# Attention probabilities of one head in four transposed by TensorE in float32, instead of by DMA in float16

## Chip, core and metric

One core of a Trainium2 chip runs the whole kernel. The metric is the device time of one execution in microseconds (us), the median over several runs. "TensorE" is the matmul engine (PE in the profile, PEld its weight loads), VectorE is DVE, ScalarE is ACT, GpSimd is POOL; SP is the engine whose queue issues most DMAs (SPq).

## What is computed

One layer of a hybrid encoder block in float32: 1024 tokens and 16 meta tokens of width 1024. Two groups of heads run beside each other, a gated delta-net (a chain over chunks of tokens, forward and backward) and attention with 8 query heads of width 64 on 2 key/value heads. Their outputs go through one output projection, a norm and an MLP of width 4096. Of the attention, which the change touches, the reference says:

```python
def attend(qb):
    s = jnp.einsum('bqhgd,bkhd->bhgqk', qb, k, preferred_element_type=jnp.float32)
    p = jax.nn.softmax(s, axis=-1).astype(v.dtype)
    return jnp.einsum('bhgqk,bkhd->bqhgd', p, v)

u = rms_norm(h, norm_mix_pre[l])
proj = u @ w_in[l]
o_dn = gated_deltanet_group(dq, dk, dv, dz, db, da, ...)
o_at = axial_gqa_group(aq, ak, av, q_norm[l], k_norm[l])
mix = jnp.concatenate([o_dn, o_at], axis=-1) @ w_out[l]
h = h + rms_norm(mix, norm_mix_post[l])
```

The chip computes float32 products from pairs of a high and a low part, so that most operands exist twice.

## The kernel before

The attention works through 64 heads: 8 tiles of 128 queries, 8 heads in each; `j` is a head's place in its group of four (`g, j = divmod(h, 4)`).

- **Scores** (`qk_head`): four matmuls of 512 columns (two halves of the keys, each with KH and KL) into one of two score buffers `S` of two PSUM banks. VectorE takes the extreme of each row (L1254) and forms the bias `nb` (L1255). The score buffer is free once ScalarE has taken the exponentials out of it.
- **Softmax** (`softmax`): ScalarE writes the exponentials of a head as float32 into `p32`, a tile `t` of a ring of four (L1262), and those of the meta keys into `pm` (L1265). It casts them to float16 into `P16` (L1268); GpSimd subtracts for the first 640 columns (L1270) and VectorE for the rest (L1271) to get the low part. Then SP issues one DMA transpose of both parts into `pT` (L1274): 8 blocks of 128x128 for the high part, 8 for the low. There are four `P16` and three `pT`.
- **Weighted sum** (`pv_head`): 24 matmuls with blocks of `pT` as weights into the accumulator `o`. For the last head of each group, the meta keys' part and the division follow, and `AQ` takes the result.

Beside this stand, one after the other, the delta-net chain (`chain`: matmuls on `st`, `rr`, `tt`, `at`, `kd`), the load and split of the output projection's weights (`wout_stream`), and the projection itself (`proj_stream`: `mix` transposes a tile of both groups' outputs, then 48 matmuls of 512 columns on `wob*` and `woa*`). All these take PSUM banks from one pool `a` of three (`psr`); the scores and `o` have their own five.

The order of all this isn't written out by hand. Each stage is a generator; `progress` runs them against a clock `T.t` that counts planned TensorE time (a transpose adds 0.1 us, a matmul its columns). `yield 2.0` means "not before 2 us of planned time later", and of those due the one first in `URGENCY` goes. So a matmul or transpose that is added anywhere moves what comes behind it on all engines. Each engine then runs its own instructions strictly in that order. In planned time, the weighted sum of a head is due `TP_` = 13.8 after its scores, and the steps of `softmax` are `SM` = 1.46, 1.4, 0.7 and 2.0 apart.

Of the kernel before, what the change touches and what calls it, by code (L numbers as in the profile page):

```python
# [8 lines left out]
F16 = mybir.dt.float16  # L9
# [4 lines left out]
ALU = mybir.AluOpType  # L14
AX = mybir.AxisListType
P = 128
# [8 lines left out]
NQ = 8  # L25
# [45 lines left out]
INF, P16N = 6, 4  # L71
# [4 lines left out]
AB, GB, SB, PTB = 3, 5, 2, 3  # L76
# [5 lines left out]
def body(tc, I, out, dbg=None):  # L82
    nc = tc.nc
    V, A, G, S = nc.vector, nc.scalar, nc.gpsimd, nc.sync
# [3 lines left out]
    class Clock:  # L88

        t = 0.0  # L90
# [10 lines left out]
    T = Clock()  # L101
# [10 lines left out]
    def tmp(dt=F32):  # L112
        return tp.tile([P, LT + 4], dt, name="t4", tag="t4")

    def psr():
        return psa.tile([P, 512], F32, name="a", tag="a")

    def ps1():
        return (R["g"] or psa).tile([P, 512], F32, name="a", tag="a")
# [13 lines left out]
    def v3(ap, m=P):  # L133
        return ap.rearrange("p (h c) -> p h c", c=m)

    def cload(name, pool=cp):
        at, n = WHERE[name]
        t = pool.tile([P, n], F32, name="c_" + name, tag="c_" + name, bufs=1)
        S.dma_start(t, cst[:, at:at + n])
        return t  # L140
# [32 lines left out]
    R = dict(g=psg)  # L173
# [472 lines left out]
    idf = cload("id")  # L646
# [16 lines left out]
    ps = ps1()  # L663
# [579 lines left out]
    def qk_head(t, h, qs, sm, mm, box):  # L1243
        kv = h // 4
        ap_, KH, KL = R["at"], R["KH"], R["KL"]
        s = R["ps"].tile([P, L], F32, name="S", tag="S", bufs=SB)
        for half in range(2):
            sl = slice(half * 512, (half + 1) * 512)
            for i, K_ in enumerate((KH, KL)):
                T.matmul(s[:, sl], lhsT=qs[:, h], rhs=K_[:, kv, sl], start=i == 0, stop=i == 1)  # L1250
            if half == 0:
                yield
        mx, nb = small(1, "mx"), small(1, "nb")
        V.tensor_reduce(mx, s, AX.X, ALU.min)  # L1254
        V.tensor_scalar(nb, mx, mm[:, h:h + 1], UP15, ALU.min, ALU.add)  # L1255
        spawn("post", softmax(t, h, s, sm, nb, box))
        yield

    def softmax(t, h, s, sm, nb, box):
        yield SM[0]  # L1260
        p32 = tmp()
        A.activation(p32[:, :L], s, AF.Exp, bias=nb, scale=-1.0)  # L1262
        g, j = divmod(h, 4)
        pm = R["PM"][(2 * t + g) % 3]
        A.activation(pm[:, j * NM:(j + 1) * NM], sm[:, h * NM:(h + 1) * NM], AF.Exp, bias=nb, scale=-1.0)  # L1265
        yield SM[1]
        p16 = R["P16"][(t * NQ + h) % P16N]
        A.copy(p16[:, 0], p32[:, :L])  # L1268
        yield SM[2]
        G.tensor_tensor(p16[:, 1, :LH], p32[:, :LH], p16[:, 0, :LH], ALU.subtract)  # L1270
        V.tensor_tensor(p16[:, 1, LH:], p32[:, LH:L], p16[:, 0, LH:], ALU.subtract)  # L1271
        yield SM[3]
        pT = R["at"].tile([P, 16, P], F16, name="pT", bufs=PTB)
        S.dma_start_transpose(pT, p16.rearrange("p a b -> p (a b)"))  # L1274
        box[h] = pT
        if j == 3:
            ps = psr()[:, :P]
            T.transpose(ps, pm, idf)
            mh, ml = (R["at"].tile([P, P], F16, name=n, bufs=2) for n in ("pmh", "pml"))
            A.copy(mh, ps)  # L1280
            V.tensor_tensor(ml, ps, mh, ALU.subtract)
            box["m", g] = mh, ml
# [608 lines left out]
```

## Time and profile before

| | before |
|---|---|
| median of 3 runs | 1414.7 us (1414.13 to 1419.95) |
| the profiled execution | 1416.07 us, its span 1414.2 us |
| TensorE busy | 1342.7 us, 95% of the span |
| VectorE, ScalarE, GpSimd busy | 1029.3, 835.5, 295.4 us |
| attention in the trace | scores from 435.8 us on, last weighted sum until 745.5 us |
| end of the delta-net chain, start of the projection's matmuls | 582.7 us, 623.7 us |

Busy time of an engine is the time in which it executes; TensorE's matmuls overlap, and their ends are modelled, so that the distance from one start to the next says more than a duration. The time from one engine's wait to another's end is read from rows of the timeline, and "idle <- X" in such a row means that the engine stood until X was done. A DMA share over 1 means that packets of several transfers overlapped on the 16 rings.

### The profile page before, as it was taken

The page shows a single profiled execution, that of the slowest core. Times are in us where ns is not written, and L with a number is a line of the kernel's source. Part 1 is how long each engine was busy: PE and PEld are TensorE (multiplying, and loading weights), DVE is VectorE, ACT ScalarE, POOL GpSimd, SP SyncE. Part 2 cuts the span into 40 slices and gives each one's busy share as a digit, 9 for nine tenths or more (in the row PEclk, how much of TensorE's full clock was granted, in tenths as well). Part 3 has the DMA queues.
Part 4 walks back from the last instruction along what each step waited for, and adds up shares of the span by engine and source line. Part 5 has one row for each costly group of instructions (what it writes and reads, how often), then busy time and mean ns, then how long its engine had stood idle before and what let it go on. Part 6 is the DMA issues. An engine that isn't in the chain of part 4 may idle for free. (4 is left out here: it accounts for less than half of the span.)

```text
span 1414.2 us, 26476 instructions
## 1 busy us (share of the span) xinstructions
PE 1342.7 (95%) x9627; PEld 1027.1 (73%) x9627; DVE 1029.3 (73%) x1962; ACT 835.5 (59%) x1747; POOL 295.4 (21%) x386
## 2 busy tenths in 40 slices
PE   6999999999998998899998799999999999999996
PEld 6999888777998877677777444444444888888875
DVE  5636779788768979877765987777775588675675
ACT  6556565756546777866644676666665455445552
POOL 1210234343534456533321200000000000000000
PEclk9999999999998999889999799999999999999998
DMA  6312234344379999997994354444443984466341
GB/s 209 87 57 62 83 98 158 112 149 153 121 253 282 245 264 239 221 242 186 224 225 135 102 175 158 153 155 150 158 155 114 331 271 127 142 193 194 98 150 66
DMA packets 273355, 236.86 MB, mean 167 GB/s; under 512 B 147484, under 2 KB 201656, under 8 KB 273224
## 3 DMA queue, kind: packets, MB, share of 16 engines
q1 hardware_dynamic: 270056, 225.73, 55.3%
q10 hardware_dynamic: 3168, 9.44, 1.8%
q8 instruction: 76, 1.25, 0.4%
q14 instruction: 55, 0.45, 0.1%
HBM read 132.27 MB, written 69.28 MB: 143 GB/s over the span
## 5 line engine op out<-in xcount | busy, mean ns | idle before, releaser
L95 PEld LDWEIGHTS <-wh 128*128 128x128 f16 x896 | 88.1, 99 | 102.7 <-issue 1.9
L95 PE MATMUL a<-woah 128*128 128x512 f32 x672 | 158.6, 390 | 1.3 <-DVE woah L1734 1.2
L95 PE MATMUL a<-woal 128*128 128x512 f32 x672 | 157.4, 389 | 0.0
L95 PEld LDWEIGHTS a<-woah 128*128 128x128 f32 x672 | 125.9, 188 | 29.0 <-DVE woah L1734 2.0
L95 PEld LDWEIGHTS a<-woal 128*128 128x128 f32 x672 | 126.1, 188 | 26.2
L95 PE MATMUL a<-uh,wh 128*128 128x344 f32 (+2 forms) x340 | 122.3, 360 | 0.7 <-ACT cw L665 0.5
L1270 POOL TENSOR_TENSOR P<-t,P 128x640 f16<-128x640 f32 x64 | 99.4, 1555 | 106.8 <-ACT P L1268 85.0
L95 PE MATMUL a<-ul,wh 128*128 128x344 f32 (+2 forms) x340 | 118.7, 349 | 0.5 <-DVE ul L262 0.5
L95 PE MATMUL a<-uh,wl 128*128 128x344 f32 (+2 forms) x340 | 118.3, 348 | 0.0
L161 POOL TENSOR_TENSOR rs<-ms,mhalf 128x1 f32<-128x1 f32 (+1 forms) x33 | 19.1, 578 | 424.0 <-DVE rs L1797 304.6
L1254 DVE TENSOR_REDUCE mx<-S 128x1 f32<-128x1024 f32 x64 | 77.9, 1219 | 24.3 <-PE S L95 24.1
L1262 ACT ACTIVATE t<-S,nb 128x1024 f32<-128x1024 f32 x64 | 71.5, 1117 | 40.8 <-DVE nb L1255 29.2
L95 PEld LDWEIGHTS <-pT 128*128 128x128 f16 x1536 | 59.5, 100 | 42.0 <-issue 26.6
L95 PE MATMUL o<-VP,pT 128*128 128x65 f16 (+1 forms) x1536 | 73.6, 198 | 11.3 <-DMA pT<-P 9.8
L95 PEld LDWEIGHTS <-wl 128*128 128x128 f16 x448 | 43.9, 98 | 54.1 <-issue 1.7
L1731 ACT ACTIVATE woah<-fr,isf 128x512 fp32r<-128x512 f32 x54 | 39.2, 725 | 70.3 <-PE a L95 61.0
L1731 ACT ACTIVATE woal<-fr,isf 128x512 fp32r<-128x512 f32 x54 | 39.2, 726 | 68.4 <-PE a L95 66.2
L1268 ACT CAST P<-t 128x1024 f16<-128x1024 f32 x64 | 66.8, 1043 | 4.7 <-DVE t L269 1.8
L1733 DVE SCALAR_TENSOR_TENSOR woah<-fr,isf,woah 128x512 fp32r<-128x512 f32 x54 | 40.5, 751 | 37.2 <-ACT woah L1731 37.1
L95 PE MATMUL S<-KH,qs 128*128 128x512 f32 x128 | 61.0, 476 | 6.5 <-ACT t L1262 6.5
L95 PEld LDWEIGHTS a<-uh,wh 128*128 128x128 f32 x340 | 65.0, 191 | 2.5 <-ACT cw L665 0.7
L95 PEld LDWEIGHTS a<-ul,wh 128*128 128x128 f32 x340 | 65.1, 192 | 2.1 <-DVE ul L262 1.0
(508 smaller groups left out, 3776.8 us busy)
## 6 DMA issues: line engine op xcount, KB each, us to landing
fr<-fscr SPq DMA_DIRECT2D x108, 256.0 KB
fscr<-os SPq DMA_DIRECT2D x64, 256.0 KB
rb<-in_w_down SPq DMA_DIRECT2D x64, 256.0 KB
fscr<-of SPq DMA_DIRECT2D x48, 256.0 KB
wr<-in_w_in SPq DMA_DIRECT2D x44, 256.0 KB
AQ<-in_w_up SPq DMA_DIRECT2D x22, 512.0 KB
raw<-in_w_up SPq DMA_DIRECT2D x10, 512.0 KB
X<-in_x SPq DMA_DIRECT2D x8, 512.0 KB
```

The lines of the kernel that those rows point to most:

```text
L95: nc.tensor.matmul(out, lhsT=lhsT, rhs=rhs, **kw)
L161: G.tensor_tensor(dst, ms[:r, :n], mhalf[:r, :n], ALU.pow)
L1254: V.tensor_reduce(mx, s, AX.X, ALU.min)
L1262: A.activation(p32[:, :L], s, AF.Exp, bias=nb, scale=-1.0)
L1268: A.copy(p16[:, 0], p32[:, :L])
L1270: G.tensor_tensor(p16[:, 1, :LH], p32[:, :LH], p16[:, 0, :LH], ALU.subtract)
L1731: A.activation(ah, fr, AF.Copy, scale=isf[:, p:p + 1])
L1733: V.scalar_tensor_tensor(al, fr, isf[:, p:p + 1], ah.bitcast(F32), ALU.mult, ALU.subtract)
```

## The change

For the second head of each group of four (`j == 1`, 16 of 64) the float32 probabilities aren't cast, subtracted and sent to the DMA. TensorE transposes them from `p32`, four blocks into one PSUM bank, twice. ScalarE copies each bank as float16 into the high half of `pT`, and VectorE subtracts that copy from the bank into the low half. The other 48 heads stay as they were; the index of `P16` now counts only them.

```diff
         yield SM[1]
-        p16 = R["P16"][(t * NQ + h) % P16N]
+        if j == 1:
+            pT = R["at"].tile([P, 16, P], F16, name="pT", bufs=PTB)
+            for half in range(2):
+                ps, sl = v3(psr()), slice(4 * half, 4 * half + 4)
+                for k in range(4):
+                    T.transpose(ps[:, k], p32[:, (4 * half + k) * P:(4 * half + k + 1) * P], idf)
+                A.copy(pT[:, sl], ps)
+                V.tensor_tensor(pT[:, 8 + 4 * half:12 + 4 * half], ps, pT[:, sl], ALU.subtract)
+                yield 0.6
+            box[h] = pT
+            return
+        p16 = R["P16"][(t * 6 + h - h // 4 - (h % 4 > 1)) % P16N]
         A.copy(p16[:, 0], p32[:, :L])
```

In the changed program the copies are line 1273, the subtractions line 1274, the DMA transpose is line 1285, and all lines behind stand 11 further down.

TensorE at the first changed head (`t_6430` is its p32, `c_id` the identity, `a` a bank of the pool of three):

```order
 L95 MATMUL a<-KM,qs 128x32 x8
+L95 MATMUL S<-KH,qs 128x512
+L95 MATMUL S<-KL,qs 128x512
+L99 MATMUL a<-c_id,t_6430 128x128 x4
+L95 MATMUL S<-KH,qs 128x512
+L95 MATMUL S<-KL,qs 128x512
+L99 MATMUL a<-c_id,t_6430 128x128 x4
 L95 MATMUL a<-rr_5956,tt_5764 128x128 x4
-L95 MATMUL a<-rr_5966,tt_5774 128x128 x2
```

The two groups of four transposes now stand between the halves of a later head's scores, ahead of the chain's matmuls.

ScalarE near head 17 before (L1262 takes exponentials, L1268 casts, L1124 belongs to the chain):

```order
L1262 ACTIVATE t_7454<-S,nb 128x1024
L1124 ACTIVATE junk,so<-O_6109 128x128
L1265 ACTIVATE PM_6218<-sm__6847,nb 128x16
L1124 ACTIVATE junk,so<-O_6109 128x128
L1268 CAST P_6214<-t_7454 128x1024
L1262 ACTIVATE t_7517<-S,nb 128x1024
```

and after (L1279 is the cast, L1097 scales a result of the chain):

```order
L1262 ACTIVATE t_7509<-S,nb 128x1024
L1265 ACTIVATE PM_6218<-sm__6839,nb 128x16
L1262 ACTIVATE t_7571<-S,nb 128x1024
L1265 ACTIVATE PM_6218<-sm__6839,nb 128x16
L1279 CAST P_6214<-t_7571 128x1024
L1097 ACTIVATE O_6098<-a,dec 128x128 x4
L1273 CAST pT<-a 128x512 x2
L1097 ACTIVATE O_6109<-a,dec 128x128 x4
L1262 ACTIVATE t_7646<-S,nb 128x1024
```

The cast of head 17 is gone; its two copies stand behind the exponentials, cast and chain work that follow it in the order, and ahead of the exponentials of head 19.

SP's queue between the loads of w_out and the load of `zt`, with which `mix` of the first tile begins, before:

```order
L1327 DMA npre<-in_w_out 128x1024
L1274 DMA_TRANSPOSE pT<-P_6215 128x16x128
L1274 DMA_TRANSPOSE pT<-P_6216 128x16x128
L1274 DMA_TRANSPOSE pT<-P_6213 128x16x128
L1274 DMA_TRANSPOSE pT<-P_6214 128x16x128
L1274 DMA_TRANSPOSE pT<-P_6215 128x16x128
L1349 DMA dnw<-in_dn_out_norm 128x1
L1350 DMA npost<-in_norm_mix_post 128x1024
L1351 DMA npre<-in_norm_mlp_pre 128x1024
L1274 DMA_TRANSPOSE pT<-P_6216 128x16x128
L1369 DMA zt<-zscr 128x4x128
```

and after:

```order
L1338 DMA t_8666<-in_w_out 128x1024
L1132 DMA oscr<-O_6098 128x512
L1285 DMA_TRANSPOSE pT<-P_6216 128x16x128
L1132 DMA oscr<-O_6109 128x512
L1285 DMA_TRANSPOSE pT<-P_6213 128x16x128
L1338 DMA npost<-in_w_out 128x1024
L1338 DMA npre<-in_w_out 128x1024
L1285 DMA_TRANSPOSE pT<-P_6214 128x16x128
L1360 DMA dnw<-in_dn_out_norm 128x1
L1380 DMA zt<-zscr 128x4x128
```

Six transposes stood between the last load of w_out and `zt`. Now one does, two more stand among the loads themselves, and the loads of the two gains come behind `zt`.

## Rows read from the trace of the kernel before

**Rows 1.** Windows A, B, C: stretch, length, busy by engine, PEclk, DMA share, GB/s

```profile
435.80:582.70 146.90, 134.75 (x1513) 117.81 (x1512) 128.41 (x281) 108.65 (x225) 81.70 (x60) 0.97 1.09 245
582.70:623.70 41.00, 32.49 (x372) 25.41 (x371) 35.18 (x60) 33.14 (x60) 17.52 (x14) 0.79 1.07 244
623.70:773.20 149.50, 143.69 (x1207) 111.30 (x1206) 96.60 (x176) 80.00 (x144) 44.06 (x38) 1.00 0.82 203
```

**Rows 2.** Tile pT: its transposes (ns min/median/max); who waited for it (us, times)

```profile
L1274 SPq DMA_TRANSPOSE pT<-P x64: 1577/2545/6613, 449.1 to 730.1; - x64
...
  PEld L95: 15.0, 13
  PE o L95: 9.8, 8
```

**Rows 3.** Waits of PE in A and in B: us in total, times, longest

```profile
PE a L95 <- DVE rr L1090: 2.0, 1, 2.0
...
PE S L95 <- ACT t L1262: 5.2, 7, 1.5
```

**Rows 4.** Groups by form, whole span: count, busy us, mean ns, idle before

```profile
L1270 POOL TENSOR_TENSOR P<-t,P 128x640 f16<-128x640 f32 x64 | 99.4, 1555 | 106.8 <-ACT P L1268 85.0 <-issue 17.3 <-POOL P L1270 2.3
...
L1268 ACT CAST P<-t 128x1024 f16<-128x1024 f32 x64 | 66.8, 1043 | 4.7 <-DVE t L269 1.8 <-DVE ml L1378 1.6 <-DMA pT<-P 1.2
...
L1271 DVE TENSOR_TENSOR P<-t,P 128x384 f16<-128x384 f32 x64 | 49.6, 778 | 17.3 <-ACT P L1268 17.2
```

**Rows 5.** Timeline of PE in C: start us, us, instruction, count

```profile
686.51 0.63 PE L99 MATMUL a<-c_id,AQ 128*128 128x128 f32 x4
686.98 0.35 PE L95 MATMUL o<-VP,pT 128*128 128x65 f16 x6
...
687.53 0.48 PE L95 MATMUL S<-KH,qs 128*128 128x512 f32 x1
687.85 0.40 PE L95 MATMUL S<-KL,qs 128*128 128x512 f32 x1
...
688.31 0.40 PE L95 MATMUL S<-KL,qs 128*128 128x512 f32 x1
```

**Rows 6.** Groups by form, 745 to 805 us: copy and subtraction out of PSUM

```profile
L1437 ACT CAST b11h<-a 128x512 f16<-128x512 f32 x4 | 2.4, 590 | 1.6 <-PE a L99 1.6
...
L1438 DVE TENSOR_TENSOR b22l<-a,b22h 128x512 f16<-128x512 f32 x4 | 2.7, 684 | 0.0
```

**Rows 7.** Windows of half clock: two of four, and the sum of all

```profile
566.50:569.90 3.40, 3.40 (x24) 2.86 (x23) 3.01 (x4) 1.04 (x3) 2.49 (x3) 0.50 1.25 236
597.20:614.30 17.10, 14.23 (x122) 11.81 (x122) 13.55 (x20) 12.48 (x18) 4.81 (x4) 0.50 1.14 243
sum 27.40, PE 24.27 PEld 20.07 DVE 19.95 ACT 18.45 POOL 10.44; mean PE 6.07 PEld 5.02 DVE 4.99 ACT 4.61 POOL 2.61
```

**Rows 8.** Timeline of PE at two places in A

```profile
469.44 0.39 PE L95 MATMUL S<-KL,qs 128*128 128x512 f32 x1
...
565.77 0.45 PE L95 MATMUL o<-VP,pT 128*128 128x65 f16 x9 [1.89 <-DMA pT<-P]
```

**Rows 9.** Timeline of SP's queue in B

```profile
592.61 15.54 SPq L1274 DMA_TRANSPOSE pT<-P  x5
...
612.12 1.99 SPq L1274 DMA_TRANSPOSE pT<-P  x1
614.16 0.58 SPq L1369 DMA_DIRECT2D zt<-zscr  x1
```

**Rows 10.** Timeline of ACT: exponentials of head 9 and of head 57

```profile
474.45 1.12 ACT L1262 ACTIVATE t<-S,nb 128x1024 f32<-128x1024 f32 x1 [0.22 <-DVE nb L1255]
...
695.18 1.12 ACT L1262 ACTIVATE t<-S,nb 128x1024 f32<-128x1024 f32 x1 [0.58 <-DVE ms L160]
```

**Rows 11.** Waits of SP's queue, 440 to 740 us

```profile
SPq L1274 <- PE o L95: 35.6, 20, 3.8
```

**Rows 12.** Chain of work that ended last, a piece between projection and MLP

```profile
785.57 6.93 DMA raw<-in_w_up
```

## The prediction

> **What bounds the kernel now.** I read the windows by stage first, then the waits of TensorE in these stages, then single places. The attention falls into three stages [rows 1]: A, attention beside the delta-net chain, from the first score matmul to the chain's last (146.9 us, TensorE busy 134.75); B, attention almost alone, up to the first matmul of the output projection (41.0 us, 32.49 busy); C, attention beside that projection (149.5 us, 143.69 busy). In A and B the DMA rings are full (share 1.09 and 1.07), VectorE is busy for 128.41 of 146.9 us in A, and TensorE's clock is granted at 0.97 and 0.79. In C it is 1.00 and nothing but TensorE is near full: what its matmuls take more there, C takes.
>
> The waits say how much of A and B belongs to the DMA transposes [rows 2]: weight loads of TensorE stand for 15.0 us until a pT has landed, matmuls for 9.8. The two overlap; I take 12. The other wait in B is for a score buffer that ScalarE has not yet read, 5.2 us [rows 3]. So a dozen microseconds, not more, can come straight from transposes that are faster or fewer.
>
> **The change, part by part.** 16 of 64 heads change.
>
> *Removed.* 16 casts on ScalarE (1043 ns), 16 subtractions on GpSimd (1555) and 16 on VectorE (778) [rows 4], and 16 transposes on SP's queue. GpSimd loses 16 x 1.555 = 24.9 us; at 81.70 of 146.9 us in A it is no bound, so that alone gives nothing.
>
> *Added on TensorE.* Each such head has two groups of four float32 transposes. A group of this form starts at 686.51 and the next matmul at 686.98 [rows 5]: 0.47 us, and 32 groups are 15.0 us. A group also breaks a run: the first score matmul behind another form starts at 687.53 and its successor at 687.85, 0.32 us on, the next two come in 0.23 us each [rows 5]. So up to 0.09 x 32 = 2.9 us more; I take 16.5. The Trainium skill ("TensorE: Matmul & The Clock Gate", Part 4: PE-mode transpose) puts a transpose at about 275 ns in a kernel's context; that would be an estimate of 128 x 0.275 = 35 us, and 18.7 us more on the sum. The row disagrees: four take 0.47 us, since their starts overlap.
>
> *Added elsewhere.* Two copies out of PSUM and two subtractions per head. The same forms take 590 ns on ScalarE and 684 on VectorE [rows 6], so ScalarE gets 2 x 0.59 - 1.04 = 0.14 us per head and VectorE 2 x 0.684 - 0.778 = 0.59, 9.4 us in all. In C (VectorE 96.60, ScalarE 80.00 of 149.5 us) TensorE hides both. In A, where VectorE is 87% full, 8 heads bring 4.7 us; they cost that much if VectorE sets the pace there, and nothing if it doesn't. They widen the range and are not in the sum.
>
> By the order of the changed program 8 of the 16 heads have their transposes in A, 2 in B, 6 in C.
>
> *Given back.* (1) Of the 12 us of waits for pT some go, since a quarter of the transposes, 2545 ns of SP's queue each in the median [rows 2], goes. The other 48 heads still take that way. Between 0 and 15.0, I take 8. (2) There are four stretches of half clock, 27.4 us together [rows 7]. Two of the 3.4 us ones begin right behind a wait for pT, as the one at 566.5 behind 1.89 us before 565.77 [rows 8]. Half clock loses half of 3.4 us, so 0 to 3.4 for both; I take 2. The long one, 17.1 us in B, begins behind waits for score buffers, and I leave it. (3) In B, SP issues five transposes in 15.54 us between the loads of w_out and those of the gains, and one more ahead of zt [rows 9], which mix needs before the projection can begin. In the changed order three stand in that place, not six: 3 x 3.1 = 9.3 us at most. ScalarE also paces B, so it may be nothing; I take 5.
>
> *New waits on TensorE.* Its queue is in order, so all that stands behind a transpose waits with it: scores of later heads, the chain, the projection. (4) A transpose needs its head's exponentials. From the start of head 9's last score matmul at 469.44 [rows 8] to the end of its exponential (474.45 + 1.12) there are 6.1 us; for head 57, from 688.31 [rows 5] to 695.18 + 1.12, 8.0 [rows 10]. The order puts other matmuls in between, by the pitches of rows 5 worth an estimated 3.3 us at the shortest places (heads 1, 9, 57, 61) and up to 10 at others. So a wait is between 0 and some 4.5 us; I take 5 us over all 16. (5) A head's two groups hold two of the three PSUM banks that the chain, mix and the projection share, until ScalarE and VectorE have read them, and what follows must turn over the third. The nearest wait of today is 2.0 us for a result of VectorE, once in A [rows 3]. So 16 x 0 to 16 x 2.0 us; I take 5, near the low end, because such waits are rare today although the three banks turn over all the time. The Trainium skill ("Perfetto Trace Analysis", Matmuls) says that independent groups should rotate through different banks, so that reading one out overlaps the matmuls of the next. By that rule two held banks speak against this change, in the sense of (5). (6) The copy into pT waits for the weighted sum of three heads earlier, as there are three pT. Today SP's queue bears that wait, 35.6 us over 20 times [rows 11]; now ScalarE does for 16 heads, with exponentials behind it: 16 x 20/64 x 1.8 = 9 us. ScalarE is busy for 108.65 of 146.9 us in A, and in its order chain and softmax work stands ahead of most copies, so I cost it at nothing; uncovered it is 9.
>
> *The sum.* 16.5 - 8 - 2 - 5 + 5 + 5 = +11.5 us. What ends C later ends the kernel later: the way into the MLP runs through a load that is issued only then and is waited for during 6.93 us [rows 12]. The profiled execution took 1416.07 us (span 1414.2), 1.4 above the median 1414.7. So 1427.6 for such an execution, and a median of 1426.
>
> **The rivals.** *Faster: the full rings and SP's queue set the pace of A and B.* For it: the shares 1.09 and 1.07, and SP's transposes back to back. Against it: TensorE's own waits name them for 15.0 us at most. Its point is that all waits for pT go (-15), the half clock with them (half of 27.4, -13.7), and B gives 9, with 5 for (4) and (5): 16.5 - 15 - 13.7 - 9 + 5 = -16, 1398.5.
>
> *Level.* The returns come near their upper ends, the long half-clock stretch stays: 16.5 - 13 - 3.4 - 7 + 6 = -1, 1414.
>
> *Much slower: the third bank is missing at most of the 16 places.* At 2.0 us per changed head that is 32, with 9 for (4) and no gain in B: 16.5 - 8 - 2 + 32 + 9 = +47; at half the bank's price +31. I price it at +31, 1446.
>
> *The clock.* Today half clock begins behind waits [rows 7, 8]. If the new waits bring one more stretch like that from 597.2, it costs half of 17.1, 8.5 us: 1434. The Trainium skill (the same Part 4) says that transposes don't count as TensorE's being busy in the way matmuls do; by it this rival is likelier than I make it. No stretch of attention here has enough of them to decide.
>
> That the change doesn't do what it says is out: the built order has the 32 groups, and 48 transposes on SP.
>
> **How the numbers follow.** The sum 0.40, much slower 0.12, the clock 0.07, level 0.23, faster 0.18. A measurement of this kernel can tell about 0.5%, 7 us, from no change. Faster by over that 0.18; slower 0.58 (the sum's own range is 1419 to 1433, so nearly all of it, and the two cases above it); within 0.24. The range begins at 1404, which leaves out the larger half of the fast case, and ends at 1441, which leaves out most of the much slower one.
>
> **What would show it.** Right: groups at 0.47 us, waits for pT down to some 4 us, B shorter by 5 us and C longer by 10 or more, transposes that wait for t by some 5 us in all. Wrong on the fast side: A and B together shorter by more than 15 us and no half clock left. Wrong on the slow side: matmuls of chain or projection that wait for the new copies and subtractions at most places.

## The result and the profile after

The changed kernel took 1429.74 us in the median (1429.58 to 1432.99, 4 runs), the kernel before 1414.41 (1413.34 to 1419.95, 4 runs): 1.0106 of it, with a 95% interval of 1.0076 to 1.0136. Measured again beside the experiments, the ratio was 1.0086 (1.0068 to 1.0104). The forecast was 1426 within 1404 to 1441. The time came out close to it, but the experiments below show that this was in part luck: terms were wrong in both directions and nearly cancel.

| us | before | after |
|---|---|---|
| span of the profiled execution | 1414.2 | 1427.9 |
| A, beside the delta-net chain | 146.9 | 143.5 |
| B, until the projection's first matmul | 41.0 | 40.6 |
| C, beside the projection | 149.5 | 165.5 |
| heads whose scores are issued before A ends / B ends | 34.5 / 45.5 | 33 / 42 |

The windows of A, B and C of the kernel after, to set beside [rows 1] (columns as there: stretch, length, busy time by engine with instructions, PEclk, DMA share, GB/s):

```profile
437.40:580.90 143.50, 135.34 (x1500) 119.06 (x1499) 127.10 (x277) 101.80 (x220) 63.69 (x49) 0.98 0.91 216
580.90:621.50 40.60, 31.44 (x334) 26.30 (x332) 31.66 (x54) 31.39 (x63) 15.09 (x11) 0.79 0.85 226
621.50:787.00 165.50, 158.74 (x1383) 125.98 (x1384) 113.36 (x204) 88.75 (x162) 40.57 (x35) 0.99 0.63 168
```

A and B together lost 3.8 us and C gained 16.0. The span gained 13.7; 1.6 of it lie ahead of A, which starts at 437.40 and not at 435.80, and the lines that run there are not touched by the change. The DMA share fell from 1.09 to 0.91 in A and from 0.82 to 0.63 in C, so the rings are relieved; C doesn't get shorter by it. A part of what C gained has only moved there: 22 heads have their scores in it, where before it was 18.5.

Tile pT, to set beside [rows 2] (its instructions with ns min/median/max and first and last start; then who waited for it: us, times):

```profile
L1285 SPq DMA_TRANSPOSE pT<-P x48: 1585/2143/5373, 451.2 to 752.9; - x48
L1273 ACT CAST pT<-a x32: 569/586/623, 449.0 to 743.2; 128x512 f16<-128x512 f32 x32
L1274 DVE TENSOR_TENSOR pT<-a,pT x32: 673/680/692, 450.6 to 743.9; 128x512 f16<-128x512 f32 x32
...
  DVE pT L1274: 6.7, 5
  ACT pT L1273: 6.4, 3
...
  PE a L99: 2.1, 1
  PEld L95: 1.8, 3
  PE o L95: 1.3, 2
```

TensorE's waits for pT are mostly gone: 1.8 us for weight loads and 1.3 for matmuls, from 15.0 and 9.8; in the second profiled execution of the changed kernel (a_again) the matmuls wait 4.0. Two new waiters have come, ScalarE's copy and VectorE's subtraction. The waits of TensorE over the attention (430 to 780 us; engine, line and releaser: us in total, times, longest) show what stands in their place:

```profile
PE S L95 <- ACT t L1262: 4.5, 7, 1.2
PE o L95 <- DVE AQ L1321: 3.8, 4, 2.1
PE a L95 <- DVE t L1223: 3.7, 2, 2.3
PE a L99 <- DVE pT L1274: 2.1, 1, 2.1
...
PE a L99 <- DMA on<-oscr: 1.5, 1, 1.5
```

Apart from L1274 and the load of `on`, these are waits for ScalarE's and VectorE's ordinary work. For AQ and for t of L1223 they are longer than before (7.5 us together; before 1.0 for AQ and none for L1223), for others shorter, and over the attention TensorE's waits come to 23.3 us in all, 26.7 in a_again, where before they were 25.9. On ScalarE the new copies wait too. Its waits over the same stretch, those in which the copy stands:

```profile
ACT pT L1273 <- PE a L99: 8.3, 6, 3.1
...
ACT pT L1273 <- PE o L95: 6.4, 3, 3.0
```

and one of them in its timeline (start, us, instruction, and in brackets the idle time ahead of it with its releaser):

```profile
486.09 1.03 ACT L1279 CAST P<-t 128x1024 f16<-128x1024 f32 x1
490.13 1.07 ACT L1273 CAST pT<-a 128x512 f16<-128x512 f32 x2 [3.00 <-PE o L95]
491.08 1.13 ACT L1262 ACTIVATE t<-S,nb 128x1024 f32<-128x1024 f32 x1
```

ScalarE stands for 3.00 us because the weighted sum of three heads earlier still holds the pT into which it is to copy. The exponentials of a later head stand behind it and start without a gap once it is through. At 743.24 the same copy waits 3.14 us for its transposes, and TensorE waits at its own end of the chain, for a bank that VectorE has not yet read:

```profile
739.92 0.19 PE L95 MATMUL o<-VM,pml 128*128 128x65 f16 x1
742.21 0.99 PE L99 MATMUL a<-c_id,t 128*128 128x128 f32 x4 [2.11 <-DVE pT L1274]
743.00 1.06 PE L99 MATMUL a<-c_id,AQ 128*128 128x128 f32 x4
```

Behind that wait begins a stretch of half clock (0.50). The first of these windows and this one, with the sum over all six of the attention:

```profile
472.70:476.10 3.40, 3.40 (x17) 3.40 (x18) 2.87 (x5) 3.40 (x6) 1.40 (x1) 0.51 1.29 308
...
742.40:745.80 3.40, 3.40 (x15) 3.05 (x15) 3.02 (x5) 1.06 (x2) 0.00 (x0) 0.50 1.02 229
sum 27.20, PE 25.53 PEld 22.99 DVE 18.18 ACT 17.22 POOL 11.72; mean PE 4.25 PEld 3.83 DVE 3.03 ACT 2.87 POOL 1.95
```

27.2 us against 27.4 [rows 7]: the waits for pT went, and the half clock did not go with them. Each of the six stretches begins in, or within some 2 us behind, a wait of TensorE of 1.3 us or more, and four of these six waits are for VectorE: L1223 (twice), AQ and L1274. Over the 7 us ahead of the first one VectorE has no idle time, and the two subtractions of a changed head stand in its order ahead of L1223:

```profile
467.76 1.27 DVE L1274 TENSOR_TENSOR pT<-a,pT 128x512 f16<-128x512 f32 x2
...
471.73 0.69 DVE L1223 TENSOR_TENSOR t<-AQ,t 128x512 fp32r<-128x512 f32 x1
```

```profile
472.56 1.78 PE L95 MATMUL a<-idr,t 128*128 128x128 f32 x8 [2.35 <-DVE t L1223]
```

### The profile page after: what moved, and what is told of

Read it like the earlier page. It is cut to its first block, busy times and chain, and to the rows that moved or that the text cites. A ratio compares the mean times of both kernels' runs of the same rounds, so it can differ in the third digit from the quotient of the medians.

```text
span 1427.9 us, 26638 instructions
## 1 busy us (share of the span) xinstructions
PE 1357.6 (95%) x9755; PEld 1045.4 (73%) x9755; DVE 1041.3 (73%) x1978; ACT 835.6 (59%) x1763; POOL 270.3 (19%) x370
## 5 line engine op out<-in xcount | busy, mean ns | idle before, releaser
L1262 ACT ACTIVATE t<-S,nb 128x1024 f32<-128x1024 f32 x64 | 71.6, 1121 | 59.5 <-DVE nb L1255 34.5
L1281 POOL TENSOR_TENSOR P<-t,P 128x640 f16<-128x640 f32 x48 | 74.9, 1561 | 130.7 <-ACT P L1279 91.9
L95 PEld LDWEIGHTS a<-uh,wl 128*128 128x128 f32 x340 | 65.2, 192 | 1.5
L1744 DVE SCALAR_TENSOR_TENSOR woal<-fr,isf,woal 128x512 fp32r<-128x512 f32 x54 | 40.5, 749 | 34.2 <-ACT woal L1742 34.2
```

What stands on the lines that cost most here:

```text
L95: nc.tensor.matmul(out, lhsT=lhsT, rhs=rhs, **kw)
L1744: V.scalar_tensor_tensor(al, fr, isf[:, p:p + 1], ah.bitcast(F32), ALU.mult, ALU.subtract)
```

## The experiments

Ratios are to the kernel before on the same chip, with 95% intervals; 0.1% is 1.4 us. The expectations in us start from 1414.4 for the kernel before, whose median beside these runs was 1416 to 1418, so they are compared by ratio. The theories at the start: **T**, the transposes' own TensorE time makes the loss (the prediction's largest term); **O**, the new order makes it; **W**, waits of TensorE for banks, pT and exponentials make it. A theory P and a theory H came up on the way.

| run | ratio | interval |
|---|---|---|
| changed kernel again | 1.0086 | 1.0068 to 1.0104 |
| e1, transposes twice | 1.0192 | 1.0170 to 1.0214 |
| e2, second heads left out | 0.9920 | 0.9900 to 0.9940 |
| e3, plan alone | 1.0051 | 1.0034 to 1.0069 |
| e4, first five tiles only | 1.0019 | 1.0005 to 1.0034 |
| e5, changed, old plan | 1.0102 | 1.0086 to 1.0118 |
| e6, first five tiles, old plan | 1.0009 | 0.9997 to 1.0020 |
| e8, second heads left out, old plan | 0.9965 | 0.9953 to 0.9977 |
| e9, transposes only | 0.9962 | 0.9947 to 0.9976 |
| e10, changed, four pT and three P16 | 1.0047 | 1.0029 to 1.0065 |
| e11, changed, copies later | 1.0065 | 1.0051 to 1.0080 |
| e12, before, four pT and three P16 | 1.0046 | 1.0027 to 1.0065 |

### The transposes twice

```diff
                 for k in range(4):
                     T.transpose(ps[:, k], p32[...], idf)
+                planned = T.t
+                for k in range(4):
+                    T.transpose(ps[:, k], p32[...], idf)
+                T.t = planned
```

> Each group of four transposes is issued twice into the same bank, and the planned time is set back so that the plan stays that of the changed kernel; copies, subtractions and waits for exponentials stay. Theory T (the transposes' own TensorE time is the loss): 32 more groups of 0.41 to 0.47 us, +13 to +15 us on the changed kernel's 1429.7, so 1443 to 1445. Rival O (the new planned order is the loss, not the transposes): the plan is unchanged, so 1429 to 1433. Rival W (held banks, the pT ring and waits for exponentials are the loss, and TensorE stands idle beside them): the second group fills idle time, 1430 to 1436.

1444.99 us, 1.0192: over the changed kernel 0.86 to 1.06%, 12 to 15 us. This fits T in size. But the windows of the three stages don't:

```profile
433.90:580.60 146.70, 139.97 (x1567) 124.76 (x1566) 126.80 (x277) 102.53 (x221) 64.96 (x49) 0.99 0.85 214
580.60:622.00 41.40, 31.95 (x348) 26.40 (x346) 33.72 (x58) 30.41 (x62) 14.28 (x11) 0.84 0.85 215
622.00:802.90 180.90, 168.77 (x1432) 132.91 (x1432) 112.32 (x199) 89.47 (x163) 38.72 (x36) 0.96 0.66 155
```

Ten of the 16 heads have their transposes in A and B, and these stretches are within the spread of two executions of the changed kernel (143.5 and 150.9 for A). C, with six heads and so 12 more groups at 0.47 us, some 6 us of work, is longer by 15.4. So, as far as one execution of each tells, a second dose of transposes is hidden in A and B, and in C it costs more than itself: the waits there grow (one of 3.5 us for ScalarE's L1265, with which the transpose of the meta keys' part begins), and so does half clock (0.04 of 180.9 us lost against 0.01 of 165.5, by estimate 5 to 6 us). T's sum was right for a reason it doesn't give.

### The second heads left out

```diff
         if j == 1:
             for half in range(2):
                 for k in range(4):
-                    T.transpose(...)
-                A.copy(...); V.tensor_tensor(...)
+                    T.t += 0.1
                 yield 0.6
-            box[h] = pT
+            box[h] = None            # pv_head: VP's blocks as weights
             return
```

> The second head of each four is neither cast, subtracted, sent by DMA nor transposed; its weighted sum takes blocks of VP as weights in place of pT, so the output is not the attention's. The planned time advances as in the changed kernel. So this has all of the relief and none of the added work. Theory T: the relief is the waits for pT and little else, 6 to 12 us under the kernel before: 1403 to 1409. Rival O: the new order costs by itself, 1424 to 1430. Rival W: relief is large, 15 to 25 us, and the waits of the changed kernel eat it: 1390 to 1400.

The tile `pT` and the banks of these heads go too, and their weighted sums take ready blocks of VP. 0.9920, 11.3 us less than before, within what T expected (6 to 12). This bounds all that the change can give back with its own plan; with the old plan (e8, below) the same relief is worth 5.0 us. It is far from what the fast rival wanted, 15 us of waits and 13.7 of half clock.

### The plan alone

```diff
         A.copy(p16[:, 0], p32[:, :L])
-        yield SM[2]
+        if j == 1:
+            for half in range(2):
+                T.t += 0.4           # in four steps
+                yield 0.6 if half == 0 else SM[2] - 0.6
+        else:
+            yield SM[2]
```

> The kernel before, with the planned time advanced by 0.4 us twice for each second head as if it had transposes; all heads still go by DMA and no instruction is added. Theory T: within 4 us of the kernel before, 1410 to 1419. Rival O: most of the loss of the changed kernel, 1424 to 1430. Rival W: as T.

1.0051 (1.0034 to 1.0069), 5 to 10 us more than before; set against 1414.4 that is 1421.6, outside T's range and short of O's (the median as measured, 1426.17, would lie in O's, but the kernel before had 1417.85 beside it). The order is not neutral when all heads still go by DMA. In this kernel TensorE waits for pT longer than before (15.9 against 9.8 us, [rows 2]):

```profile
PE o L95 <- DMA pT<-P: 15.9, 8, 2.7
```

That led to a theory **P**: the planned time of the transposes moves some three heads from A and B, where TensorE waits anyway, into C, where it doesn't.

### The change for the first five tiles, and three kernels with the old plan

e4_ab has `if j == 1 and t < 5`, the heads in A and B. In e5, e6 and e8 the planned time is set back (`T.t = planned` behind the transposes; in e8 it isn't advanced at all). The builder still places a few rows in its own way, but the heads stand at 34.5 and 45 to 45.5 again.

> The change for the first five tiles of queries only (10 of the 16 heads; in the changed kernel those transposed beside the delta-net chain and between chain and projection); the last three tiles as before. Theory T: 10 heads cost 9.4 us of TensorE and get back the waits for pT (9.8 us before), so 1412 to 1418. If instead each head costs the same wherever it stands, 10/16 of +15.3: 1424. Rival W: the new waits are where chain and scores share the banks, 1422 to 1428.

> The changed kernel once more, to stand beside the other three on the same chip. All theories: 1.0106 of the kernel before, within its interval of 1.0076 to 1.0136.

> The changed kernel with the planned time set back after each group of transposes, so that the plan is that of the kernel before (34.5 heads' scores ahead of the chain's end and 45 ahead of the projection, not 33 and 42). Nothing is added or removed. Theory P (formed on the miss at e3_plan: the planned time of the transposes moves some 3 heads from stages in which TensorE waits into the projection's, where it doesn't): 3.5 heads were 6.6 us of nominal work in C, of which A and B gave back about 2, so 4 to 7 us less than the changed kernel: 0.995 to 0.997 of it, some 1.006 to 1.008 of the kernel before. Theory T (TensorE's added work alone): as the changed kernel within 2 us. Rival W: more work pressed between chain and scores makes the bank and pT waits longer, 2 to 6 us more than the changed kernel.

> The change for the first five tiles of queries only, as in e4_ab, and the planned time set back after each group. Theory P: 3 to 6 us less than e4_ab, which was 1.0019 of the kernel before, so 0.998 to 1.000 of the kernel before. Theory T: as e4_ab, 1.001 to 1.003. Rival W: 1.004 to 1.007.

> As e2_none (second heads neither cast, subtracted, sent by DMA nor transposed, VP's blocks as weights of their sums, so the output is not the attention's), but with the planned time of the kernel before. All relief, no added work, no new order. Theory P: 4 to 7 us less than e2_none, which was 0.992 of the kernel before, so 0.987 to 0.989. Theory T: as e2_none, 0.990 to 0.994. Rival W expects nothing else here.

e4_ab came to 1.0019 and e6 to 1.0009: ten heads out of 16 cost 1 to 3 us in all. So the other six, in C, cost 0.67 to 0.87% with the new plan and 0.93% with the old, 9.5 to 13 us, some 1.6 to 2.2 us a head where a head's two groups take 0.94. e4's ratio is within T's forecast and against W's: chain and scores, which share the banks in A, hardly suffer.

Theory P fell. e5 was no faster than the changed kernel (1.0102 against 1.0086, intervals that overlap), and e8 was slower than e2 (0.9965 against 0.9920), where P wanted both 4 to 7 us faster. With the old plan fewer heads stand in C, and yet C is 164.5 us long; TensorE waits there for pT again:

```profile
PE o L95 <- DMA pT<-P: 3.5, 2, 2.3
```

The new plan costs 7 us without the relief, is worth 6 with all of it, and makes no difference in the changed kernel. Plan and relief don't add; why is not settled.

### The transposes without copies and subtractions

```diff
                     T.transpose(ps[:, k], p32[...], idf)
-                A.copy(pT[:, sl], ps)
-                V.tensor_tensor(pT[...], ps, pT[:, sl], ALU.subtract)
                 yield 0.6
-            box[h] = pT
+            box[h] = None            # pv_head: VP's blocks as weights
```

> The changed kernel without its copies and subtractions out of PSUM and without pT for second heads: only the transposes are left of what was added; the sums of these heads take blocks of VP as weights, so the output is not the attention's. It lies between e2_none (0.992 of the kernel before) and the changed kernel (1.0086 and 1.0106 in two studies). Theory T (TensorE's own work is what the change adds): 0.992 and 13 to 15 us of transposes and a bit, close to the changed kernel, 1.001 to 1.004 at the least and 1.006 to 1.010 if they also bring half clock. Theory H (the copies and subtractions stand at the head of ScalarE's and VectorE's queues until transposes and pT's ring let them go, and exponentials and casts behind them come late): 1.000 to 1.003, and the other 6 to 10 us come with the copies.

0.9962 (0.9947 to 0.9976), below what any theory had written down. Over e2 it is 0.42%: where nothing else is added, all 128 transposes cost **5.9 us** (by the two intervals, some 2 to 9), not 16.5. The step from here to the changed kernel is 1.24 to 1.44%: copies, subtractions and the pT of 16 heads, with the sums that wait for them, cost **17.5 to 20 us**. A, B and C of e2 and then of e9:

```profile
435.20:568.00 132.80, 124.18 (x1412) 109.58 (x1411) 115.99 (x260) 93.40 (x204) 63.99 (x49) 0.99 1.01 235
568.00:607.60 39.60, 29.02 (x391) 22.94 (x389) 32.87 (x57) 29.40 (x58) 14.48 (x11) 0.91 0.96 234
607.60:765.30 157.70, 152.22 (x1288) 117.36 (x1289) 98.90 (x186) 83.27 (x151) 39.92 (x35) 0.99 0.68 176
```

```profile
435.00:575.30 140.30, 132.53 (x1476) 117.54 (x1475) 114.21 (x260) 94.17 (x204) 65.56 (x49) 0.98 0.92 228
575.30:613.40 38.10, 29.84 (x407) 24.53 (x406) 31.91 (x54) 29.55 (x58) 15.21 (x11) 0.96 0.99 232
613.40:771.70 158.30, 155.45 (x1337) 121.59 (x1338) 101.37 (x189) 83.39 (x151) 39.17 (x35) 1.00 0.70 178
```

In these executions TensorE's busy time in C rises by 3.2 us and the length by 0.6. Set beside the changed kernel's windows above, C is 7.2 us shorter, VectorE has 12.0 us less in it and ScalarE 5.4, and VectorE has 12.9 less in A. So what the last step adds is work of the two engines that read the banks and that everything else in the attention goes through. TensorE gets no instruction more by it, and yet it is busy for 8.4 us longer (the changed kernel, then e9; whole span):

```profile
PE 1357.6 (95%) x9755; PEld 1045.4 (73%) x9755; DVE 1041.3 (73%) x1978; ACT 835.6 (59%) x1763; POOL 270.3 (19%) x370
```

```profile
PE 1349.2 (96%) x9755; PEld 1036.3 (73%) x9755; DVE 1016.3 (72%) x1946; ACT 819.2 (58%) x1731; POOL 271.1 (19%) x370
```

By its size that is the clock: half clock in the attention is 27.2 us in the changed kernel and 10.2 in e9, and half of the difference is 8.5. All runs agree with the profiled ones: the mean granted clock is 0.975 to 0.981 in the ten of the changed kernel (mean 0.978) and 0.984 to 0.991 in the six of e9 (0.986). By an estimate from these, 8 to 11 of the 17.5 to 20 us are TensorE at half clock, behind the waits that the added work brings.

e9 also asks less of the ring of pT: without the 16 of the second heads, SP's queue stands 11.1 us for weighted sums, in the changed kernel 47.7, before 35.6 [rows 11]:

```profile
SPq L1282 <- PE o L95: 11.1, 7, 2.7
```

```profile
SPq L1285 <- PE o L95: 47.7, 18, 5.8
```

Part of the 17.5 to 20 us may therefore be the ring's, and the next runs look at that.

### Four pT, and copies later

```diff
-INF, P16N = 6, 4
-AB, GB, SB, PTB = 3, 5, 2, 3
+INF, P16N = 6, 3
+AB, GB, SB, PTB = 3, 5, 2, 4
```

> The changed kernel with four pT and three P16 instead of three and four (there is no room for four of both; with 48 heads on that way three P16 turn over as often as four did for 64). ScalarE's copies waited 6.4 us over 3 times for the weighted sum that frees their pT. Theory H: 3 to 7 us less than the changed kernel, 1.004 to 1.008 of the kernel before. Theory T: as the changed kernel, 1.008 to 1.011. If the P16 are short now, slower than the changed kernel, 1.011 to 1.015.

> The kernel before with four pT and three P16, the same edit as in e10_ptb4, which took 0.4 to 0.6% off the changed kernel. In e10 SP's queue stood 17.4 us for weighted sums that free a pT, in the changed kernel 47.7, in the kernel before 35.6. If the short ring is a cost of any kernel of this kind: 0.994 to 0.997 of the kernel before, since its waits for pT (9.8 us) mostly go. If it is a cost of the change (16 pT are taken earlier, from the transposes on, and a P16 is free only because 48 heads use it): 0.999 to 1.001, or 1.002 to 1.010 where three P16 are short for 64 heads and the casts wait for the DMA.

1.0047 for the changed kernel with four pT, 0.39 to 0.59% less than with three, 5.5 to 8 us: theory H. The trace (its execution took 1427.52 us, the second longest of nine) shows that it isn't ScalarE's own wait that went, as expected, but SP's (first row: SP's wait; second: ScalarE's in e10, 6.4 us before the edit):

```profile
SPq L1285 <- PE o L95: 17.4, 8, 4.3
```

```profile
ACT pT L1273 <- PE o L95: 5.5, 3, 2.7
```

My reading of these rows: a head that is transposed by TensorE takes its pT where the transposes stand, ahead of the heads' DMA, and holds it until its weighted sum; in a ring of three the other heads' DMA transposes then start later. No run tests this reading by itself. The gain shows again in the clock, 0.985 in the mean over nine runs against 0.978, by estimate 10 us. The same edit makes the kernel before slower, 1.0046, because 64 heads run short of three P16: the cast waits for the DMA for 21.4 us (before: 1.2, 2 times).

```profile
ACT P L1268 <- DMA pT<-P: 21.4, 17, 2.9
```

So the fourth pT is affordable only with the change, where fewer heads use P16; whether it alone would help the kernel before stays open, since there is no room for four of both. With this split of the buffers, the two kernels take the same time (1.0047 and 1.0046), but both more than the kernel before.

```diff
-                A.copy(pT[:, sl], ps)
+                yield 0.6
+                A.copy(pT[:, sl], ps)
                 V.tensor_tensor(pT[...], ps, pT[:, sl], ALU.subtract)
-                yield 0.6
```

> The changed kernel with each copy and subtraction written 0.6 us of planned time behind its transposes instead of right behind them. ScalarE's copies waited 8.3 us over 6 times for transposes. Theory H: they wait less and 2 to 6 us come back, 1.005 to 1.008. Rival B (held banks): banks stay taken longer and matmuls of chain and projection wait, 1.010 to 1.015. Theory T: no difference, 1.008 to 1.011.

1.0065 (1.0051 to 1.0080), on H's side by 3 to 6 us, with an interval that touches the changed kernel's; rival B, held banks, would have been slower. ScalarE's copies wait as long as they did (9.1 us for transposes, 7.2 for weighted sums), so the reason that H gave isn't shown. What differs most in the trace (of its fastest execution) is B:

```profile
577.10:615.00 37.90, 27.79 (x333) 22.63 (x331) 32.45 (x53) 31.16 (x63) 15.41 (x11) 0.91 0.92 243
```

37.9 us at a clock of 0.91 against 40.6 at 0.79. Over all runs the clock is 0.982 against 0.978, by estimate 5 us, the size of the gain.

No run here beats the kernel before with the attention whole; e6 is level with it. The fourth pT and the later copies were not tried on e6 or e4.

## Why the prediction came out near

**The bound.** Right for A and B, that DMA transposes hold TensorE there for a dozen us and no more: with all relief and no cost, e2 is 11.3 us faster. Incomplete in one point: it took C, where nothing but TensorE is near full, to pay for every matmul. In the executions of e2 and e9 C paid 0.6 us for 3.2 us more of TensorE's busy time, and A and B together 6.0.

**TensorE's transposes, +16.5.** The term that missed most, as far as the runs price it. The size of a group was right: what follows a group starts 0.79 us behind 742.21 at half clock, so some 0.4 at full, and TensorE's busy time over the span rose by 14.9 us, near the forecast. That this all lies on the path did not hold where transposes alone were added: from e2 to e9 the busy time rose by 13.8 us and the kernel's time by 5.9. Beside the copies and subtractions they are dearer, 12 to 15 us for a second dose (e1), so the term has no single price, and what the first dose costs in the changed kernel was not measured by itself. The figure of the Trainium skill that the prediction weighed against it ("TensorE: Matmul & The Clock Gate", Part 4: PE-mode transpose; about 275 ns for one, measured there in bf16) agrees with the duration of one here, 273 ns, but not with what a further one adds: 128 of them at that price would be an estimated 35 us.

**Waits for pT, -8.** Right in itself: the matmuls' 9.8 us fell to 1.3, in a second execution to 4.0. But other waits took their place, and all of TensorE's together hardly fell.

**Half clock, -2.** Wrong, it stayed at 27.2, and over all runs the granted clock went from 0.981 to 0.978. It isn't the transposes alone that keep it: e9 has all of them and only these stretches:

```profile
446.70:450.10 3.40, 3.40 (x13) 2.81 (x14) 3.08 (x6) 1.82 (x3) 3.28 (x3) 0.50 0.85 315
514.90:518.30 3.40, 3.40 (x27) 3.07 (x26) 1.50 (x4) 0.00 (x0) 1.15 (x1) 0.50 1.27 313
600.30:603.70 3.40, 3.40 (x29) 3.21 (x26) 2.49 (x4) 1.44 (x3) 0.00 (x0) 0.50 1.01 212
```

10.2 us, against 13.6 in e2 without transposes and 27.2 in the changed kernel. Over all runs the clock is 0.986 in e9 and 0.983 in e2. The clock rival drew on a rule of the Trainium skill ("TensorE: Matmul & The Clock Gate", Part 4: PE-mode transpose), that transposes don't count as TensorE's being busy in the way matmuls do; by it e9 should have gained no clock over e2, and these rows show none of its effect. What the rival feared came in part: new waits brought half clock, six stretches in place of four, but of the same total.

**B, -5.** Half right in mechanism, wrong in size. zt was issued at 602.28, not 614.16 [rows 9], but B stayed at 40.6. What TensorE waited for instead is the load of `on`, the other input of `mix`, behind a transpose that held SP's queue for 4.80 us:

```profile
602.28 0.43 SPq L1380 DMA_DIRECT2D zt<-zscr  x1
...
607.89 4.80 SPq L1285 DMA_TRANSPOSE pT<-P  x1
612.75 0.57 SPq L1382 DMA_DIRECT2D on<-oscr  x1
```

```profile
615.78 0.80 PE L99 MATMUL a<-c_id,on 128*128 128x128 f32 x4 [1.49 <-DMA on<-oscr]
```

That wait is 1.49 us, B's half clock is as long as before (17.0 and 17.1 us), and it holds a wait of 2.15 us for AQ; how these share the missing 5 us is not shown. The prediction asked what would be late next only of ScalarE, not of the second load or of VectorE.

**Waits for exponentials (4), +5, and held banks (5), +5.** Both nearly absent as named. The group of the changed transposes' weight loads (count; busy, mean ns; idle before with its releasers):

```profile
L99 PEld LDWEIGHTS a<-c_id,t 128*128 128x128 f32 x128 | 15.0, 145 | 4.6 <-DVE pT L1274 2.2 <-DVE t L1425 0.7 <-ACT t L1262 0.4
```

They waited 0.4 us for their exponentials, `t` of L1262, in all 16 heads, and the one wait for a held bank of more than 1 us is that at 742.21. So the 10 us were priced for waits that did not come; others, for late ScalarE and VectorE, did.

**The wait for pT on ScalarE (6), 0 or 9 if uncovered.** Here the prediction set a cost to nothing that it had seen. The row was read rightly (6.4 us of such waits came), but ScalarE was called covered because its busy share was 74% and other work stands ahead of most copies. In its order, a copy that waits holds a later head's exponentials. The widened work of VectorE, 9.4 us, was left out of the sum in the same way, by a busy share. These two and the ring lie within the 17.5 to 20 us behind e9; how much is each one's is not shown. By the estimate above about half of it is half clock, which the prediction had as a return.

So the sum of +11.5 was -15 of returns, +16.5 of TensorE and +10 of waits on TensorE; the runs give -11.3, +5.9, and +17.5 to 20 of copies, subtractions and ring. Counted in this order, TensorE was priced 10.6 us too high; the returns were 3.7 too good and the rest 7.5 to 10 too low. These nearly cancel: that the total was right is luck as far as this ledger goes. Another order of adding could split it otherwise, as e1 and e8 show that the parts don't simply add.

The much slower rival is nearest in C, where a changed head costs about twice its transposes' own time, but not by its mechanism, a missing third bank at most of the 16 places: that shows once, and ten heads are nearly free.

## What to carry to other kernels

A busy share doesn't price added work: on an engine busy for 95% of the span, 13.8 us more of busy time cost 5.9 here, and leaving out the other added instructions and timing the rest told so. A PSUM-to-SBUF copy in the middle of an in-order queue is to be priced by what it waits for and by what stands behind it: one of 0.6 us stood for 3.0 here. Ask of every late result whether TensorE waits for it, and look at the granted clock behind that wait. When a transfer is replaced on a few heads, look at the ring of buffers that both ways share: who takes a buffer earlier may take it from the other.

## What the runs showed that was not expected

Two executions of the same changed kernel put A at 143.5 and 150.9 us with spans of 1427.9 and 1431.0. Part of it is the clock, 0.98 and 0.94:

```profile
434.10:585.00 150.90, 139.66 (x1500) 122.86 (x1499) 128.66 (x277) 102.70 (x221) 64.09 (x49) 0.94 0.89 209
```

So stages of single executions can't be compared to better than some 7 us here, and the ratios of repeated runs, and not single windows, carry the sums above. Also, four float32 transposes of 128x128 are followed by the next matmul after 0.36 to 0.47 us, under half of four times their shown duration of 273 ns.
